# Banded attention on one core: scores and transposes in half arrays, values by pairs of key blocks, engine orders written by hand

## The chip, the cores and the metric

The kernel runs on one core of a Trainium2 chip. The metric is the device time of one execution in microseconds. The core has five engines that run at the same time: TensorE (PE, matrix products into PSUM, 8 banks of 512 fp32 columns by 128 partitions), VectorE (DVE), ScalarE (ACT), GpSimd (POOL) and SyncE (SP, which here only issues DMAs). A matmul keeps one operand in the array (the weights, which a load instruction brings in) and streams the other (the moving operand) past it.

## The reference

Two sequences (2048 and 512 rows of 1024 channels) go through an attention layer, a Fourier layer and a last RMS norm. Cut to the attention layer, which is what the change touches:

```python
def attention_layer(x, g, w_in, w_out, sink, rel_bias):
    h = rmsnorm(x, g)
    z = h @ w_in                      # q (16 heads x 64), k and v (4 heads x 64), gate (1024)
    o = banded_gqa_with_sink(q, k, v, rel_bias, sink)
    return x + (o * jax.nn.silu(gate)) @ w_out

def banded_gqa_with_sink(q, k, v, rel_bias, sink):      # blocks of 128 queries, 3 blocks of 128 keys
    scores = einsum(q, k) * scale + bias                # bias by relative position; |i - j| <= 128
    m = maximum(max(scores), sink)
    p = exp(scores - m)
    p = p / (sum(p) + exp(sink - m))
    return einsum(p, v)
```

Everything is in fp32. The kernel holds most operands as a high part, which the array's fast fp32 format keeps exactly, and a low part, the rest. A product of two such operands is three matmuls (high by high, high by low, low by high), which `matmul3` issues (lines 95 to 97).

## The kernel before

The rows are worked on in five chunks of 512 (the short sequence first). For each chunk the kernel makes the normalised and transposed input `h`, projects k and v (`kv_proj`), and then goes through 8 pairs of heads `p`. For each pair it projects q and the gate (`qg_proj`: 8 steps each, a step being one `matmul3` of 512 columns, names `qp` and `gp`) and attends (`attention`). After the last pair comes the output projection (`out_proj`, tiles `op` and `wo`). The Fourier phase follows the five chunks.

Attention of a pair goes through 4 query blocks `b` and 2 heads `j`, 64 times a chunk (`i`). For each:

- `scores` (line 436): the 128 rows of the stationary operand hold q's high part in one half and its low part in the other, so that two matmuls over 128 rows (`kwin` high, `kwin` low, the keys being held twice) make the scores of one head, 128 queries by up to 384 keys, in one of two PSUM banks `spt`. DVE adds the bias and takes the minimum of the negated scores (line 448), ACT takes the exponential and its sum (line 452), DVE the reciprocal (line 455), and DVE scales (line 458; in the first chunk ACT does so for `j` = 1, line 461).
- `transp`, `LAG` = 3 places later (line 475): up to three transposes of 128 by 128 through a PSUM tile `pt`; ACT writes the high part (line 476), DVE the low part (line 477) of the tile `pts`.
- `av`, `AVLAG` = 2 places after that (line 489): for each of up to three key blocks and for the high and the low part, a matmul of 256 columns (both heads of one query block).
- `out_evac`, once for two query blocks: ACT copies half of the result (line 497), DVE adds the halves (line 506), POOL multiplies by the gate (line 508), ACT and POOL make the high and low part of `uT` (lines 509, 510).

Between these stand the next pair's projection steps, an equal share at each place, so that TensorE has work while DVE and ACT deal with the scores. The order on an engine is the order in which the program names the instructions, as far as a scheduler leaves it; a few are tied to others with `after`. Six PSUM banks are handed out in turn (`bank`), two are `spt`. In the Fourier phase these two become a pool of their own for the accumulators W and Z.

In the first chunk the weights also come from memory in one piece and are split into high and low part on ACT (line 116) and POOL, and q and gate are scaled by the norm in PSUM (`scaled`, line 274). Later chunks read the split weights back.

## Time and profile before

| | |
|---|---|
| median of 3 runs | 1643.32 us (1642.83 to 1645.25) |
| profiled execution, its own time | 1642.68 us |
| span of its profile | 1640.9 us |
| mean granted clock of TensorE | 0.999 |
| instructions | 25865, of which 8939 matmuls |
| share of the span: PE, weight loads, DVE, ACT, POOL | 99, 85, 73, 54, 27% |
| attention stages (first to last score) | 47.1 to 185.8, 265.0 to 409.5, 482.6 to 632.6, 705.7 to 855.6, 922.6 to 1066.7 us |

The groups of the profile are named by line, engine and operation, then output tile and input tiles, the array's rows and columns, the shape, how often, the busy time, the mean length of one in ns, and the idle time before it with what ended it. A row of the order in time has the start, the length (of several equal instructions together, where it ends in x2 or more), the engine, line and tiles. Lengths of matmuls include their way through the array and overlap.

### The profile page before, as it was taken

To read this page: it belongs to the slowest core of one execution; us is meant where nothing else is said; L and a number is where in the kernel's file an instruction comes from. 1 tells how busy PE (TensorE), PEld (TensorE's weight loads), DVE (VectorE), ACT (ScalarE), POOL (GpSimd) and SP (SyncE) were. 2 spreads that over 40 slices of the span, in tenths; PEclk is the share of its full clock that TensorE was granted. 3 is DMA by queue.
4 is the path that set the end of the run, shared out by engine and by line. 5 is a ranking of instruction groups with operands and counts; after the bars stand their busy time and mean duration, and the time that the engine had idled before them with its cause. 6 is when DMAs were issued, how large, how long until landed. Compare 5 with 4: busy or idle time off the path is not lost.

```text
span 1640.9 us, 25865 instructions
## 1 busy us (share of the span) xinstructions
PE 1625.6 (99%) x8939; PEld 1400.8 (85%) x8939; DVE 1197.3 (73%) x2846; ACT 892.1 (54%) x2035; POOL 434.9 (27%) x605
## 2 busy tenths in 40 slices
PE   9999999999999999999999999999999999999998
PEld 7888888888898888988888888888888888888886
DVE  6778665888548886478783588858667667988696
ACT  6789644676236674256761467636545454343252
POOL 2457641422403313224214142121111111100010
PEclk9999999999999999999999999999999999999999
DMA  8487786574866556765648755657565469655962
GB/s 303 157 316 292 233 327 218 193 250 168 285 224 232 186 206 204 270 242 173 224 149 318 249 197 193 222 191 253 198 238 192 172 221 390 215 193 187 336 212 90
DMA packets 100637, 374.05 MB, mean 228 GB/s; under 512 B 12139, under 2 KB 22379, under 8 KB 83100
## 3 DMA queue, kind: packets, MB, share of 16 engines
q1 hardware_dynamic: 81708, 297.91, 52.7%
q0 software_dynamic: 16464, 70.30, 11.0%
q10 hardware_dynamic: 2336, 4.20, 0.7%
q8 instruction: 71, 1.16, 0.3%
q14 instruction: 58, 0.48, 0.1%
HBM read 281.10 MB, written 91.26 MB: 227 GB/s over the span
## 4 chain that ended last, share of the span: by engine, by line
PE 88%; DMA 4%; DVE 3%; ACT 2%; POOL 1%; issue 1%; SPq 0%; POOLq 0%; DVEq 0%; ACTq 0%
PE av L489 6%; PE spt L436 6%; PE pt L475 6%; PE gp L95 4%; PE gp L97 4%; PE gp L96 4%; PE qp L95 4%; PE qp L97 4%; PE qp L96 4%; PE op L95 4%; PE op L97 4%; PE op L96 4%; PE W L95 2%; PE W L96 2%; PE W L97 2%; PE fo L96 2%
## 5 line engine op out<-in xcount | busy, mean ns | idle before, releaser
L452 ACT ACTIVATE S<-S 128x385 f32<-128x385 f32 (+1 forms) x320 | 190.8, 596 | 68.9 <-DVE S L448 67.4
L477 DVE TENSOR_TENSOR pts<-pt,pts 128x384 fp32r<-128x384 f32 (+1 forms) x320 | 168.3, 526 | 41.1 <-ACT pts L476 38.8
L448 DVE CUSTOM_DVE_ANT_0 S<-spt,b 128x385 f32<-128x385 f32 (+1 forms) x320 | 168.1, 526 | 25.5 <-PE spt L436 23.3
L476 ACT CAST pts<-pt 128x384 fp32r<-128x384 f32 (+1 forms) x320 | 143.6, 451 | 76.1 <-PE pt L475 72.7
L436 PE MATMUL spt<-kwin,qab 128*128 128x384 f32 (+1 forms) x640 | 156.8, 326 | 0.0
L508 POOL TENSOR_TENSOR o<-o,s 128x256 f32<-128x256 f32 x75 | 55.4, 739 | 362.9 <-DVE o L506 361.2
L475 PE MATMUL pt<-ident,S 128*128 128x128 f32 x896 | 150.5, 273 | 0.1
L436 PEld LDWEIGHTS spt<-kwin,qab 128*128 128x128 f32 x640 | 118.3, 188 | 25.4 <-DVE S L448 0.2
L489 PEld LDWEIGHTS av<-pts,v 128*128 128x128 f32 x896 | 126.3, 189 | 13.6 <-DVE qab L382 1.3
L95 PE MATMUL gp<-h,wg 128*128 128x512 f32 x320 | 137.8, 431 | 0.0
L489 PE MATMUL av<-pts,v 128*128 128x256 f32 x896 | 136.4, 285 | 1.0 <-DVE qab L382 0.5
L95 PE MATMUL qp<-h,wq 128*128 128x512 f32 x312 | 133.7, 428 | 0.5 <-ACT wq L116 0.5
L95 PE MATMUL op<-wo,uT 128*128 128x512 f32 x320 | 126.5, 397 | 1.5 <-ACT invb L177 0.9
L475 PEld LDWEIGHTS pt<-ident,S 128*128 128x128 f32 x896 | 113.8, 140 | 14.5 <-DVE pts L477 3.4
L97 PE MATMUL gp<-h,wg 128*128 128x512 f32 x320 | 125.9, 393 | 0.0
L96 PE MATMUL gp<-h,wg 128*128 128x512 f32 x320 | 125.7, 393 | 0.0
L96 PE MATMUL op<-wo,uT 128*128 128x512 f32 x320 | 125.7, 393 | 0.0
L97 PE MATMUL op<-wo,uT 128*128 128x512 f32 x320 | 124.7, 391 | 0.0
L458 DVE TENSOR_SCALAR S<-S 128x384 f32<-128x384 f32 (+1 forms) x256 | 118.6, 463 | 7.9
L97 PE MATMUL qp<-h,wq 128*128 128x512 f32 x312 | 123.0, 394 | 0.1
L96 PE MATMUL qp<-h,wq 128*128 128x512 f32 x312 | 122.6, 393 | 0.0
L455 DVE RECIPROCAL S<-S 128x1 f32<-128x1 f32 x320 | 51.3, 160 | 65.9 <-ACT S L452 63.0
(420 smaller groups left out, 4261.0 us busy)
## 6 DMA issues: line engine op xcount, KB each, us to landing
wo<-wsd SPq DMA_DIRECT2D x32, 1024.0 KB, 5.8
wq<-wsd SPq DMA_DIRECT2D x31, 1024.0 KB, 5.1
wg<-wsd SPq DMA_DIRECT2D x31, 1024.0 KB, 6.8
x<-x1d SPq DMA_DIRECT2D x40, 512.0 KB, 3.9
b<-b21d SPq DMA_DIRECT2D x40, 512.0 KB, 5.5
b<-rowd SPq DMA_DIRECT2D x40, 384.0 KB, 4.3
xs<-in_x_dram SPq DMA_DIRECT2D x23, 512.0 KB, 6.0
s2d<-gt POOLq DMA_DIRECT2D x40, 256.0 KB, 3.7
```

Source lines behind the costliest of these rows:

```text
L95: PE.matmul(out, a[0], b[0], start=start, stop=False, skip_group_check=more)
L96: PE.matmul(out, a[0], b[1], start=False, stop=False, skip_group_check=more)
L97: PE.matmul(out, a[1], b[0], start=False, stop=stop, skip_group_check=more)
L436: PE.matmul(ps[:, 2 + k0 * P : 2 + k1 * P], q, kwin[g][:, part, b * P + k0 * P : b * P + k1 * P], start=part == 0, stop=part == 1,)
L448: DVE.tensor_tensor_reduce(out=s[:, e0:e1], in0=ps[:, 1 + e0 : 1 + e1], in1=st["bias"][:, j, 386 - e1 : 386 - e0][:, ::-1], scale=1.0, sca ...
L452: last_exp[0] = ACT.activation(s[:, e0:e1], s[:, e0:e1], AF.Exp, bias=mn, scale=-1.0, accum_out=den)
L458: DVE.tensor_scalar(s[:, ks], s[:, ks], den, None, ALU.mult)
L475: PE.transpose(ps[:, kb, :], s[:, 1 + kb * P : 1 + (kb + 1) * P], ident)
L476: ACT.copy(hi[:, k0:k1, j, :], ps[:, k0:k1, :])
L477: DVE.tensor_tensor(lo[:, k0:k1, j, :], ps[:, k0:k1, :], f32(hi[:, k0:k1, j, :]), ALU.subtract)
L489: PE.matmul(out, v, pt[:, kb].rearrange("p h q -> p (h q)"), start=kb == k0 and part == 0, stop=kb == k1 - 1 and part == 1,)
L508: eng.tensor_tensor(o, o, s, ALU.mult)
```

## The change

- A period is now two query blocks of one pair of heads, 16 to a chunk and one more to empty the pipeline. In period `n` the scores of its two blocks are made, and the transposes, values and evacuation belong to period `n` - 1.
- `scores` makes three products per head, each over 64 rows: head 0 in the first 64 rows of the array, head 1 in the other 64, in turn. q is evacuated in one piece for both heads (high part on ACT, low part on DVE). There are three `spt` banks in place of two.
- `transp` is split in halves of 64 queries: the moving operand is a 64 by 64 identity, the stationary one 64 rows of the probabilities by 128 keys. The two halves use the two halves of the array and two PSUM banks.
- On TensorE the order of a period is: scores of the first block, all half transposes of the period before, scores of the second block (these three in 64 rows), projection steps, values, projection steps.
- `av` works on both query blocks at once: the two key blocks that both of them see take matmuls of 512 columns, the outer two take 256.
- For `j` = 1 ACT does the scaling in all chunks, for `j` = 0 DVE.
- The order on PE, ACT and DVE is tied by `seq`, each instruction behind the one before it. The number of projection steps at each place is a list, `quota`.
- The pool of banks has 5 in place of 6. The first half of the output projection uses the three `spt` banks and one of the pool; k is projected into `spt`. In the Fourier phase W, Z and X share a pool of three.

The diff, cut to its core:

```diff
+    def seq(engine, ins):
+        after(ins, chain.get(engine))
+        chain[engine] = ins
+        return ins
...
-                    qa, qb = qab[:, 0], qab[:, 1]
-                    ACT.activation(qa[0:64], ps[0:64], AF.Copy, scale=-0.125)
-                    DVE.scalar_tensor_tensor(qa[64:128], ps[0:64], -0.125, f32(qa[0:64]), ALU.mult, ALU.subtract)
-                    ACT.activation(qb[64:128], ps[64:128], AF.Copy, scale=-0.125)
-                    DVE.scalar_tensor_tensor(qb[0:64], ps[64:128], -0.125, f32(qb[64:128]), ALU.mult, ALU.subtract)
+                    seq(ACT, ACT.activation(qab[:, 0], ps, AF.Copy, scale=-0.125))
+                    lo = DVE.scalar_tensor_tensor(qab[:, 1], ps, -0.125, f32(qab[:, 0]), ALU.mult, ALU.subtract)
+                    seq(DVE, lo)
...
-                    for part in range(2):
-                        PE.matmul(
-                            ps[:, 2 + k0 * P : 2 + k1 * P],
-                            q,
-                            kwin[g][:, part, b * P + k0 * P : b * P + k1 * P],
-                            start=part == 0,
-                            stop=part == 1,
-                        )
+                    for i, (qp, kp) in enumerate(((0, 0), (0, 1), (1, 0))):
+                        for j in range(2):
+                            rows = slice(64 * j, 64 * j + 64)
+                            pe(PE.matmul(
+                                banks[j][:, 2 + k0 * P : 2 + k1 * P],
+                                res["q"][rows, qp, b * P : (b + 1) * P],
+                                kwin[g][rows, kp, b * P + k0 * P : b * P + k1 * P],
+                                start=i == 0,
+                                stop=i == 2,
+                            ))
...
-                    for kb in range(k0, k1):
-                        PE.transpose(ps[:, kb, :], s[:, 1 + kb * P : 1 + (kb + 1) * P], ident)
-                    ACT.copy(hi[:, k0:k1, j, :], ps[:, k0:k1, :])
-                    DVE.tensor_tensor(lo[:, k0:k1, j, :], ps[:, k0:k1, :], f32(hi[:, k0:k1, j, :]), ALU.subtract)
+                    for j in range(2):
+                        for kb in range(k0, k1):
+                            for h in range(2):
+                                rows = slice(64 * h, 64 * h + 64)
+                                pe(PE.transpose(
+                                    ps[h][:, kb, j, :], ss[j][rows, 1 + kb * P : 1 + (kb + 1) * P], ident[rows, rows]
+                                ))
+                def parts(b):
+                    gb, k0, k1 = span(b)
+                    for h, ps in enumerate(st.pop(("pt", b))):
+                        hi, lo = (st["pts"][:, i, b % 2, k0:k1, :, 64 * h : 64 * h + 64] for i in range(2))
+                        seq(ACT, ACT.copy(hi, ps[:, k0:k1]))
+                        seq(DVE, DVE.tensor_tensor(lo, ps[:, k0:k1], f32(hi), ALU.subtract))
...
+                    todo = [(gb, slice(1, 4, 2), by_b), (gb + 1, slice(2, 5, 2), by_b)]
+                    if k0 == 0:
+                        todo.append((gb - 1, 0, out[:, :256]))
+                    if k1 == 3:
+                        todo.append((gb + 2, 5, out[:, 256:]))
+                    for n, (kb, at, to) in enumerate(todo):
+                        v = vblk[kb][:, g].rearrange("p a d -> p (a d)")
+                        for part in range(2):
+                            pt = pts[:, part].rearrange("p b k h q -> p (b k) (h q)")[:, at]
+                            pe(PE.matmul(to, v, pt, ...))
...
-                        st["ps"] = [bank(f"op{c}_{half}_{i}") for i in range(4)]
+                        st["ps"] = (spt if half == 0 else []) + [bank(f"op{c}_{half}_{i}") for i in range(3 * (1 - half), 4)]
...
+                ahead_n = 16 if c == 0 else 12
...
+                m = 15 * KD - ahead_n
+                quota = [m * (i + 1) // 27 - m * i // 27 for i in range(27)] + [3, 3, 2]
...
+                for n in range(17):
+                    new = (at[n // 2], 2 * (n % 2)) if n < 16 else None
+                    old = (at[(n - 1) // 2], 2 * ((n - 1) % 2)) if n else None
...
+                    if new:
+                        new[0].scores(new[1], spt[:2])
+                    if old:
+                        for b in range(2):
+                            old[0].transp(old[1] + b)
+                    if new:
+                        for j in range(2):
+                            new[0].biased(new[1], j)
+                        new[0].scores(new[1] + 1, (spt[2], spt[0]))
+                    if old:
+                        for b in range(2):
+                            old[0].parts(old[1] + b)
+                    if new:
+                        for j in range(2):
+                            new[0].exps(new[1], j)
+                        for j in range(2):
+                            new[0].biased(new[1] + 1, j)
+                    for i in range(quota[2 * n] if n < 15 else 0):
+                        work.pop(0)()
+                    if n >= 15:
+                        for i in range(n - 14):
+                            op.pop(0)()
+                    if new:
+                        new[0].divide(new[1], 0)
+                        for j in range(2):
+                            new[0].exps(new[1] + 1, j)
+                    if split:
+                        split()
...
+                    if old:
+                        old[0].av(old[1])
+                    if new:
+                        new[0].divide(new[1], 1)
+                        new[0].divide(new[1] + 1, 0)
+                    if old:
+                        split = old[0].out_evac(old[1])
+                    if new:
+                        new[0].divide(new[1] + 1, 1)
...
+                    if n < 15:
+                        for i in range(quota[2 * n + 1]):
+                            work.pop(0)()
+                    elif n == 15:
+                        op.pop(0)()
+                    else:
+                        split()
+                        for i in range(3):
+                            op.pop(0)()
```

More of the change, by code (lines that the diff above doesn't have):

```diff
@@ L93, in matmul3 @@
     def matmul3(out, a, b, start, stop, more=False):
-        PE.matmul(out, a[0], b[0], start=start, stop=False, skip_group_check=more)
-        PE.matmul(out, a[0], b[1], start=False, stop=False, skip_group_check=more)
-        PE.matmul(out, a[1], b[0], start=False, stop=stop, skip_group_check=more)
+        for i, j in ((0, 0), (0, 1), (1, 0)):
+            pe(PE.matmul(out, a[i], b[j], start=start and i + j == 0, stop=stop and i == 1, skip_group_check=more))
     def load_w(c, n, name, lo_engine=None, late=None):
@@ L126, in load_w @@
         return w[:, 0], w[:, 1]
[L128 removed]
+    stage, res_tile, ready, chain = [], [], {}, {}
     def after(ins, anchor):
@@ L259, in attention_phase, with zeros @@
             spt = []
-            for i in range(2):
-                s = spsum.tile([P, 512], F32, name=f"spt{i}")
-                DVE.memset(s, 0.0)
-                spt.append(s)
+            for i in range(3):
+                spt.append(spsum.tile([P, 512], F32, name=f"spt{i}"))
+            def zeros(s):
+                for cs in (slice(0, 2), slice(386, 388)):
+                    DVE.memset(s[:, cs], 0.0)
             kall = ap.tile([P, 4, 2, 768], F32R, align_bytes=LINE, name="kwin")
@@ L305, in cols @@
                     return h[0][:, c0 : c0 + n], h[1][:, c0 : c0 + n]
-                kps = [bank(f"kp{c}_{t}")[:, :n] for t in range(2)]
+                kps = [spt[1 + t][:, :n] for t in range(2)]
                 for k in range(KD):
@@ L355, in kv_proj @@
                         evac_k(t, pt[:, t * P : t * P + P], P, CH + P)
+                for t in range(3):
+                    zeros(spt[t])
                 return invb
@@ new lines, in transp @@
+                    if b % 2 == 0:
+                        st["pts"] = ap.tile([P, 2, 2, 3, 2, P], F32R, align_bytes=LINE, tag="pt", bufs=1, name=f"pts{c}_{p}_{b}")
+                    ps = st["pt", b] = [
+                        bank(f"pt{c}_{p}_{b}_{h}")[:, :384].rearrange("p (k j q) -> p k j q", k=3, j=2) for h in range(2)
+                    ]
+                    for j in range(2):
[4 more added lines that the diff above has]
+                                    ps[h][:, kb, j, :], ss[j][rows, 1 + kb * P : 1 + (kb + 1) * P], ident[rows, rows]
+                                ))
@@ L575, in out_proj @@
                 return steps
+            Heads = namedtuple("Heads", "start scores biased exps divide transp parts av out_evac")
             def pieces(out, a, b, op):
@@ L691, in attention_phase @@
             AHEAD = ahead()
-            HB = [(b, j) for b in range(4) for j in range(2)]
             tail = []
             bias = []
+            norm_steps = invb = inv = None
             def first_norms():
@@ L770, in attention_phase @@
+                chain.pop(PE)
+                if c == len(CHUNKS) - 1:
+                    for i in range(2):
+                        op[i]()
+                        op[i] = lambda: None
+                tail = op
             return tail
```

228 lines of the change are left out of this document (105 added, 123 removed).

## The prediction

> **What bounds the kernel now.** I read the page first, then the busy time by stage, then the groups of TensorE, then the order of time in one attention stage.
>
> ```profile
> span 1640.9 us, 25865 instructions
> ## 1 busy us (share of the span) xinstructions
> PE 1625.6 (99%) x8939; PEld 1400.8 (85%) x8939; DVE 1197.3 (73%) x2846; ACT 892.1 (54%) x2035; POOL 434.9 (27%) x605
> ```
> ```profile
> 47.10:185.80 138.70, 136.21 (x777) 116.94 (x776) 112.51 (x388) 119.56 (x293) 78.38 (x113) 1.00 0.67 245
> 705.70:855.60 149.90, 149.90 (x860) 130.90 (x858) 126.68 (x379) 100.39 (x252) 43.66 (x59) 1.00 0.59 198
> ```
> The two rows are the attention stages of the first and the fourth chunk (columns: length, then PE, weight loads, DVE, ACT, POOL). TensorE is busy for 149.9 of 149.9 us. DVE has 85% in the later chunk, ACT 86% in the first. So a stage is as long as the sum of TensorE's slots, and a change is worth what it takes off that sum, less the waits that it brings.
>
> Matmuls overlap: the printed length of one is not its share of the time. The share is the distance between starts.
>
> ```profile
> L475 PE MATMUL pt<-ident,S 128*128 128x128 f32 x896 | 150.5, 273 | 0.1
> ...
> L489 PE MATMUL av<-pts,v 128*128 128x256 f32 x896 | 136.4, 285 | 1.0 <-DVE qab L382 0.5 <-DVE pts L477 0.4
> ...
> L436 PE MATMUL spt<-kwin,qab 128*128 128x384 f32 x512 | 131.3, 337 | 0.0
> ...
> L436 PE MATMUL spt<-kwin,qab 128*128 128x256 f32 x128 | 25.5, 282 | 0.0
> ```
> ```profile
> 719.60 0.40 PE L97 MATMUL gp<-h,wg 128*128 128x512 f32 x1
> 719.84 0.51 PE L436 MATMUL spt<-kwin,qab 128*128 128x384 f32 x2
> 720.18 0.49 PE L475 MATMUL pt<-ident,S 128*128 128x128 f32 x3
> 720.43 0.48 PE L95 MATMUL gp<-h,wg 128*128 128x512 f32 x1
> 720.74 0.39 PE L96 MATMUL gp<-h,wg 128*128 128x512 f32 x1
> 720.97 0.40 PE L97 MATMUL gp<-h,wg 128*128 128x512 f32 x1
> ```
> The next rows, from the start of the run, are needed for 256 columns now and for more below:
>
> ```profile
> 17.21 0.39 PE L96 MATMUL kp<-h,wk 128*128 128x512 f32 x1
> 17.43 0.39 PE L97 MATMUL kp<-h,wk 128*128 128x512 f32 x1
> 17.75 1.03 PE L249 MATMUL bp<-oh,rb 33*16 33x512 f32 x2
> 18.71 0.38 PE L95 MATMUL vp<-wv,h 128*128 128x256 f32 x1
> 18.93 0.28 PE L96 MATMUL vp<-wv,h 128*128 128x256 f32 x1
> 19.05 0.28 PE L97 MATMUL vp<-wv,h 128*128 128x256 f32 x1
> ```
> Two scores last 0.51 with a mean of 0.337, so they start 0.174 apart. Three transposes last 0.49 with 0.273 each: 0.109 apart. A 512-column product follows the next after 0.23. For 256 columns (18.93 to 19.05) it is 0.12.
>
> **The change on TensorE, part by part.**
>
> Scores. Before: 512 x 0.174 + 128 x 0.12 = 104.4 us. After, a head takes three products in its own 64 rows, and the two heads of a pair stand in the two halves of the array. There are 960 matmuls, 480 pairs (384 wide, 96 narrow). If a pair costs one slot: 384 x 0.174 + 96 x 0.12 = 78.3. **-26.1 us.**
>
> Values. Before 896 x 0.12 = 107.5. After, 320 matmuls of 512 columns and 256 of 256: 320 x 0.23 + 256 x 0.12 = 104.3. **-3.2 us.**
>
> Transposes. Before 896 x 0.109 = 97.7; after 1792 halves with 64 moving columns, 896 pairs. What bounds one now is told by the one plain fp32 matmul of the trace, bp at 17.75 above, in the answer on its tile:
>
> ```profile
> L249 PE MATMUL bp<-oh,rb x2: 589/594/600, 17.8 to 18.2; 33*16 33x512 f32 x2
> ```
> Its two passes of 512 fp32 columns take 1.03 together and one 0.59, so they start 0.44 apart; a quarter of that is 0.110, the slot of a transpose. So the 128 moving fp32 columns set it, and 64 need 0.055. I take 0.06 per pair, near that end; the other end is 0.109, where the weight load of 128 columns, which the halving doesn't shorten, is the limit. 896 x 0.06 = 53.8: **-43.9 us** (-48 to 0).
>
> Switches. The new order has the 64-row work of a period in one stay: scores, 24 half transposes, scores. That is 17 stays in each of 5 chunks, so 170 switches, where before has one pair of them, at bp, which uses part of the rows. The weight loads there:
>
> ```profile
> 17.75 0.11 PEld L249 LDWEIGHTS bp<-oh,rb 33*16 33x16 f32 x2 [0.35 <-issue]
> 18.71 0.19 PEld L95 LDWEIGHTS vp<-wv,h 128*128 128x128 f32 x1 [0.85 <-ACT xs L155]
> 18.82 0.19 PEld L96 LDWEIGHTS vp<-wv,h 128*128 128x128 f32 x1
> ```
> Into it: 0.32 from the last kp to bp, against 0.23: 0.09, and its weight load started with it, not ahead (16 columns; a load of 128 prints 0.10 longer, 0.19 against some 0.09). Out of it: 18.71 - 18.19 = 0.52 against 0.44, then 0.22 against 0.12 for the first vp, whose load was not ahead: 0.18. So 0.09 to 0.19 each. I take 0.17, near the upper one, as the first loads here have 128 columns: 170 x 0.17 = **+28.9 us** (+15 to +32). The Trainium skill (TensorEngine Tiling (Array Packing), Key Properties) says that a change of tiling mode drains TensorE, and this is the rule that speaks against the change; it gives no price, and the rows here agree that there is one.
>
> Waits at the end of a chunk. In the fixed order, work is handed out as 8 projection steps to a period, but periods 13 and 14 (of 0 to 16) have 7 and 5, and in period 15 the step behind the second scores is the output projection, whose first product goes into spt0: the bank of the scores that were written last. DVE must first do two biased sums, the four low parts of the earlier transposes and two more sums:
>
> ```profile
> L448 DVE CUSTOM_DVE_ANT_0 S<-spt,b 128x385 f32<-128x385 f32 x63 | 34.9, 554 | 5.1 <-PE spt L436 4.7
> L477 DVE TENSOR_TENSOR pts<-pt,pts 128x384 fp32r<-128x384 f32 x60 | 33.2, 553 | 2.5 <-ACT pts L476 2.1
> ...
> L506 DVE TENSOR_TENSOR o<-av,t 64x256 f32<-64x256 f32 x28 | 11.7, 416 | 0.7 <-ACT t L497 0.4
> L455 DVE RECIPROCAL S<-S 128x1 f32<-128x1 f32 x62 | 10.0, 161 | 13.1 <-ACT S L452 12.5
> L393 DVE SCALAR_TENSOR_TENSOR s<-th,gp 128x512 f32<-128x512 f32 x8 | 5.5, 686 | 1.1 <-ACT th L391 1.1
> ```
> 4 x 0.554 + 4 x 0.553 = 4.4 us, in which TensorE has 12 pairs of halves (0.72), three of scores (0.52) and a switch: 1.4. It then waits 3.0. In period 14 the last gate's evacuation (0.69 on DVE) also stands in front of the next sums, with three steps fewer (3 x 3 x 0.23 = 2.1 us) to cover it: 1 more. **4 us x 5 chunks = +20** (+5 to +30: instructions of an engine overlap a little at their ends).
>
> Waits inside. ACT's queue in a period: four high parts, two exponentials, the evacuation of q or gate, two exponentials, uT, one normalising copy, the copy of av, another normalising copy.
>
> ```profile
> L452 ACT ACTIVATE S<-S 128x385 f32<-128x385 f32 x63 | 38.9, 618 | 16.9 <-DVE S L448 16.9
> L476 ACT CAST pts<-pt 128x384 fp32r<-128x384 f32 x60 | 28.1, 472 | 10.9 <-PE pt L475 10.2
> L452 ACT ACTIVATION_READ_ACCUMULATOR S<-S 128x1 f32 x63 | 11.9, 188 | 0.0
> L497 ACT COPY t<-av 64x512 f32<-64x512 f32 x14 | 8.2, 583 | 1.0 <-PE av L489 0.7
> ```
> Estimated from these, a normalising copy (384 wide, like the exponential) and an evacuation (512 wide, like the copy of av) are 0.6 each and uT (256 wide) 0.4. This makes 4 x 0.806 + 4 x 0.472 + 0.583 + 3 x 0.6 + 0.4 = 7.9 us. TensorE's period is 6 x 0.174 + 12 x 0.06 + 1.4 + 24 x 0.23 + 0.34 = 9.0. It holds, with little room where chunk 0 adds a weight's cast to each period. DVE, which gives half of its scaling to ACT, has about the same. The q evacuation halves on both (two 64-row pieces become one of 128). I put **+5 us** (0 to 10). The five banks of the pool, three banks for scores, and X of the Fourier stage in a pool of three only exchange places; the work between covers their release, 0.
>
> Sum: -26.1 - 3.2 - 43.9 + 28.9 + 20 + 5 = -19.3. The profiled execution took 1642.7 (its span of 1640.9 and 1.8 around it), 0.6 under the median of three: 1642.7 - 19.3 = 1623.4, and **1624.0** against the median.
>
> **The rivals.**
>
> *The fixed order becomes the bound* (slower). The last block's transposes need the second normalising copy, which stands behind the copy of av, two adds (0.416 each) and a reciprocal (0.161). ACT comes to the copy of av after the evacuation, two exponentials, uT and a normalising copy: 0.6 + 1.6 + 0.4 + 0.6 = 3.2 us after the first projection steps land, 1.8 after av does. From there 0.58 + 0.83 + 0.16 + 0.6 = 2.2, so it is ready 4.0 after av; TensorE gets there after 12 products (2.75), a switch and 0.52 + 0.54: also 4.0. Any ACT work in that stretch then stalls it. The first chunk has these:
>
> ```profile
> L116 ACT CAST wq<-w32q 128x1024 fp32r<-128x1024 f32 x5 | 5.2, 1046 | 0.0
> ```
> ```profile
> L274 DVE TENSOR_TENSOR gp<-gp,invb 128x512 f32<-128x512 f32 x8 | 5.5, 683 | 0.9 <-PE gp L97 0.9
> ```
> 1.05 + 0.68, of which I let 0.2 hide: 1.5 x 16 = 24 us; and half of the other 64 periods have a split of a later weight (512 wide, about 0.6, 0.4 of it bare): 13. 1624 + 37 = **1661**. It decides from 0.25 us a period on (20 / 80). Against it: instructions of ACT overlap, so 7.9 is an upper sum. Chance 0.22.
>
> *The halves' weight loads queue.* The loads above start 0.11 apart (18.71, 18.82). If two halves share that path, a pair of scores takes 0.22, 480 x 0.22 - 78.3 = +27, and a pair of transposes at least today's 0.109, +44: **1695**; at 0.22 it is +143, 1794. For it: no row shows two loads at once. Chance 0.13. The Trainium skill (TensorE: Matmul & The Clock Gate, LDWEIGHTS) says that a load's time goes by its columns and not by its rows, 107 ns for 128; by that alone, with the loads one behind the other, it would be the 1794. The Trainium skill (TensorEngine Tiling (Array Packing), Key Properties) also says that different tiles load and multiply in parallel, and then it is not. No run so far shows either.
>
> *The halves do not run side by side at all.* Scores 768 x 0.174 + 192 x 0.12 = 156.7 in place of 78.3, transposes 1792 x 0.06 = 107.5 in place of 53.8: 1624 + 132 = **1756**. Chance 0.10. That the order isn't the one described can be left out: the built program has the 170 switches and 1376 matmuls in either half.
>
> **How the numbers follow.** The forecast has 0.55; its own range is 1594 (pair 0.055, switch 0.09, ends at 2 us) to 1660 (pair 0.09). The whole range, 1594 to 1697, takes in the fixed order's case and the queue's lower price; beyond it lie the third rival and the queue's upper price. Faster by over 0.2% (3.3 us, about what a measurement can tell here): 0.50 of the forecast and 0.03 of the first rival; same 0.06; slower 0.41.
>
> **What would show it.** Right: score pairs 0.17 apart, halves of a transpose almost together and pairs about 0.06 apart, 0.1 to 0.2 around each stay, a gap of 2 to 5 us before the first output projection product into spt0. Wrong: slots of 0.17 for single scores, 0.11 for pairs of transposes, TensorE waiting in the middle chunks for ACT's normalising copies, or an attention stage that is longer than 150 us in the fourth chunk.

## The result, and the profile after

| | before | after |
|---|---|---|
| median of 4 runs each | 1644.03 us (1642.83 to 1645.25) | 1711.99 us (1707.01 to 1715.54) |
| span of the profiled execution | 1640.9 us | 1705.2 us |
| mean granted clock of TensorE | 0.999 | 0.983 |

The changed kernel is slower by 4.1% (ratio 1.0411, 95% interval 1.0383 to 1.0439). The forecast was 1624; the range ended at 1697.

The head of the page after (the last row is TensorE's granted clock in tenths of full speed, in 40 equal slices of the run):

```profile
span 1705.2 us, 27749 instructions
...
PE 1632.8 (96%) x9835; PEld 1348.5 (79%) x9835; DVE 1104.6 (65%) x2703; ACT 918.6 (54%) x2123; POOL 437.5 (26%) x605
...
PEclk9988999999999999999999999999999999999999
```

TensorE had 99% before. It now stands idle for 4% of a longer span, its clock is lower in places, and no engine beside it is busier than 65% (the weight loads are TensorE's own). So nothing ran out of throughput; something waits. The attention stages of the first and the fourth chunk (same columns as in the prediction):

```profile
42.20:205.70 163.50, 143.00 (x918) 110.61 (x917) 115.77 (x374) 113.60 (x284) 77.19 (x112) 0.93 0.58 204
751.80:898.20 146.40, 140.35 (x1017) 111.57 (x1016) 101.80 (x335) 108.15 (x272) 43.88 (x58) 1.00 0.57 200
```

In the first chunk TensorE is idle for 20 us and its clock is 0.93; in the fourth it is idle for 6 us inside the stage, where before it was idle for none. The stage itself looks 3.5 us shorter, but it holds less: the three steps of the output projection that stood inside it before (37 products, 8.5 us) now come behind the last score, against one more projection step inside (2.7 us).

A period in which nothing waits shows what the half arrays cost and bring (order of time, fourth chunk, TensorE; start, length):

```profile
807.69 0.79 PE L441 MATMUL spt<-kwin,qab 64*128 64x384 f32 x6
808.31 0.92 PE L499 MATMUL pt<-ident,S 64*128 64x64 f32 x24
809.03 0.88 PE L441 MATMUL spt<-kwin,qab 64*128 64x384 f32 x6
809.85 3.02 PE L95 MATMUL gp<-h,wg 128*128 128x512 f32 x12
812.70 1.54 PE L525 MATMUL av<-pts,v 128*128 128x512 f32 x8
814.08 2.91 PE L95 MATMUL qp<-h,wq 128*128 128x512 f32 x12
816.92 0.61 PE L441 MATMUL spt<-kwin,qab 64*128 64x384 f32 x3
```

From start to start: first scores 0.62, 24 half transposes 0.72 (0.06 a pair), second scores 0.82, projection 2.85, values 1.38, projection 2.84: 9.23 us. The halves do run side by side. A later period, 30 us on, has the waits. ACT, DVE and TensorE in it:

```profile
835.11 0.62 ACT L680 CAST e<-w32e 128x512 fp32r<-128x512 f32 x1
835.63 0.62 ACT L478 ACTIVATE S<-S 128x384 f32<-128x384 f32 x1
836.27 0.58 ACT L534 COPY t<-av 64x512 f32<-64x512 f32 x1
838.45 0.62 ACT L478 ACTIVATE S<-S 128x384 f32<-128x384 f32 x1 [1.59 <-DVE S L476]
```
```profile
837.31 0.85 DVE L543 TENSOR_TENSOR o<-av,t 64x256 f32<-64x256 f32 x2 [1.68 <-ACT t L534]
838.19 0.16 DVE L476 RECIPROCAL S<-S 128x1 f32<-128x1 f32 x1
```
```profile
836.78 0.78 PE L441 MATMUL spt<-kwin,qab 64*128 64x384 f32 x6
837.40 0.59 PE L499 MATMUL pt<-ident,S 64*128 64x64 f32 x13
838.30 0.37 PE L499 MATMUL pt<-ident,S 64*128 64x64 f32 x5 [0.31 <-DVE o L543]
839.12 0.41 PE L499 MATMUL pt<-ident,S 64*128 64x64 f32 x6 [0.45 <-ACT S L478]
```

This is one chain through three queues. ACT's cast of a later weight (835.11) holds up the copy of the values (836.27). DVE, which has nothing to do but must add before it may take the reciprocal, waits 1.68 us for that copy. ACT waits 1.59 us for the reciprocal, and TensorE's last six half transposes wait for ACT's normalising copy; five others wait for the adds, because these free the bank they write. Over the run, in the table of waits (total us, times, longest):

```profile
ACT S L478 <- DVE S L476: 101.3, 88, 3.6
DVE o L543 <- ACT t L534: 94.3, 69, 5.7
PEld pt L499 <- ACT S L478: 29.2, 61, 0.6
PE pt L499 <- DVE o L543: 12.8, 16, 1.2
PE spt L95 <- DVE S L460: 10.8, 5, 2.4
PE spt L441 <- DVE S L460: 9.9, 10, 2.0
```

For sums over the run I take the distance between the starts of successive matmuls less the slot of the first one's width, and count only waits of over 0.2 us. By that TensorE waits 46 us between transposes (77 places), 16.5 at the scores (most of it for the bank `spt0` between the two blocks, some for the low part of q), 12 before the first product of the output projection (about 2.4 in each chunk), 90 in all; before it was 11.

The clock is the second part. Before, it is 1.0 until the run's end. After, it is 0.5 in eleven stretches of 3.41 or 6.83 us, 54.6 us together, which make the slots in them longer by 17.7 us. Busy time by windows around two of them (length, PE, PEld, DVE, ACT, POOL, clock):

```profile
436.00:439.40 3.40, 0.79 (x5) 0.47 (x5) 3.40 (x13) 2.10 (x7) 0.00 (x0) 1.00 0.32 135
439.40:442.80 3.40, 3.36 (x8) 2.68 (x9) 1.13 (x7) 1.72 (x6) 0.73 (x1) 0.50 0.61 153
...
1019.66:1023.07 3.41, 1.76 (x32) 1.31 (x28) 2.13 (x8) 2.12 (x5) 3.41 (x6) 1.00 0.34 138
1023.07:1026.48 3.41, 3.41 (x12) 2.66 (x9) 2.68 (x10) 2.12 (x7) 1.59 (x3) 0.50 0.37 154
```

The first holds the wait before an output projection, the second two waits at transposes:

```profile
1021.59 0.37 PE L499 MATMUL pt<-ident,S 64*128 64x64 f32 x5 [1.19 <-DVE o L543]
1022.40 0.40 PE L499 MATMUL pt<-ident,S 64*128 64x64 f32 x6 [0.45 <-ACT S L478]
```

Behind both, TensorE works through a window at half clock.

### The profile page after: what moved, and what is told of

It reads as the page before. It is cut to its first block, busy times and chain, and to the rows that moved or that the text cites. A ratio compares the mean times of both kernels' runs of the same rounds, so it can differ in the third digit from the quotient of the medians.

```text
span 1705.2 us, 27749 instructions
## 1 busy us (share of the span) xinstructions
PE 1632.8 (96%) x9835; PEld 1348.5 (79%) x9835; DVE 1104.6 (65%) x2703; ACT 918.6 (54%) x2123; POOL 437.5 (26%) x605
## 4 chain that ended last, share of the span: by engine, by line
PE 68%; ACT 9%; DVE 8%; DMA 8%; issue 4%; POOL 2%; SPq 0%; DVEq 0%; POOLq 0%; ACTq 0%
PE spt L95 8%; PE op L95 8%; PE qp L95 8%; PE gp L95 7%; PE fo L95 6%; PE W L95 6%; PE vp L95 3%; PE z L95 3%; PE spt L441 3%; ACT S L478 3%; PE Z L95 3%; PE Wo L95 2%; PE av L525 2%; DVE o L543 2%; PE pt L499 2%
## 5 line engine op out<-in xcount | busy, mean ns | idle before, releaser
L95 PE MATMUL gp<-h,wg 128*128 128x512 f32 x960 | 244.4, 403 | 0.0
L95 PE MATMUL qp<-h,wq 128*128 128x512 f32 x960 | 241.0, 401 | 0.0
L95 PEld LDWEIGHTS gp<-h,wg 128*128 128x128 f32 x960 | 178.4, 192 | 45.1 <-issue 10.3
L95 PEld LDWEIGHTS qp<-h,wq 128*128 128x128 f32 x960 | 178.2, 191 | 42.4 <-issue 5.2
L478 ACT ACTIVATE S<-S 128x384 f32<-128x384 f32 (+1 forms) x160 | 95.0, 595 | 102.8 <-DVE S L476 101.3
L95 PE MATMUL op<-wo,uT 128*128 128x512 f32 x600 | 142.6, 389 | 0.0
L441 PE MATMUL spt<-kwin,qab 64*128 64x384 f32 (+1 forms) x960 | 129.4, 362 | 13.0 <-DVE S L460 9.9
L95 PE MATMUL fo<-wo,tTu 128*128 128x512 f32 x576 | 138.9, 392 | 0.0
L95 PEld LDWEIGHTS op<-wo,uT 128*128 128x128 f32 x600 | 112.7, 188 | 23.6
L543 DVE TENSOR_TENSOR o<-av,t 64x256 f32<-64x256 f32 x150 | 62.6, 417 | 102.2 <-ACT t L534 94.3
L95 PEld LDWEIGHTS fo<-wo,tTu 128*128 128x128 f32 x576 | 106.0, 188 | 20.2
L525 PE MATMUL av<-pts,v 128*128 128x512 f32 (+1 forms) x576 | 118.7, 345 | 2.5 <-ACT pts L507 1.9
```

The costliest lines, as they stand in the source:

```text
L95: pe(PE.matmul(out, a[i], b[j], start=start and i + j == 0, stop=stop and i == 1, skip_group_check=more))
L441: pe(PE.matmul(banks[j][:, 2 + k0 * P : 2 + k1 * P], res["q"][rows, qp, b * P : (b + 1) * P], kwin[g][rows, kp, b * P + k0 * P : b * P + k ...
L478: seq(ACT, ACT.activation(s[:, ks], s[:, ks], AF.Copy, scale=den))
L525: pe(PE.matmul(to, v, pt, start=n == part == 0, stop=part == 1 and n in (1, len(todo) - 1), skip_group_check=n > 1,))
L543: seq(DVE, DVE.tensor_tensor(o[64 * j : 64 * j + 64], ps[0:64, :, j], t2[:, :, j], ALU.add))
```

## The experiments

Three theories. **A**: the fixed orders of ACT and DVE make the normalised scores, and the banks, late for TensorE; it waits, and after waits it runs at half clock. **B**: the half arrays themselves cost more than they save. **C**: bundles of two blocks always wait for something; what is removed at one place turns up at another. The medians are each compared with runs of the kernel before on the same chip (1643.4 to 1644.7).

**Each cause by itself, first four.** The last normalising copy goes ahead of the values' evacuation in ACT's and DVE's order:

```diff
+                    if new:
+                        new[0].divide(new[1] + 1, 1)
                     if old:
                         split = old[0].out_evac(old[1])
-                    if new:
-                        new[0].divide(new[1] + 1, 1)
```


> The changed kernel with one move: the last normalising copy of a period stands ahead of the evacuation of the values, so that it waits no longer for the copy of av and the two adds. Theory A (the fixed order of ACT and DVE is late for the transposes, and TensorE's waits then halve its clock): most of the 46 us that the transposes of the changed kernel wait inside their runs go, and with them some of the half-clock stretches: 1640 to 1670 us. Theory B (work in half arrays is itself slow, the waits are a by-product): within 10 us of 1712. Theory C (order in general: any fixed order gives as much waiting elsewhere): 1690 to 1710, with the waits moved to av or the scores.

1697.01 us (1.0333, 1.0305 to 1.0361): 15 us better. Waits between transposes fell from 46 to 40 us and those between scores from 16.5 to 9.4, but now the transposes wait for a bank:

```profile
PEld pt L499 <- ACT pts L507: 29.6, 28, 1.8
```

The chain is real, but turning the order round makes the copy of the values late, and DVE's adds with it (in this run they wait 131 us for it). Both neighbours are needed at the same time.

The output projection later in the last period (the moved calls are not shown), and its banks in another order:

```diff
-                quota = [... // 27 ... for i in range(27)] + [3, 3, 2]
+                quota = [... // 28 ... for i in range(28)] + [2, 3, 3]
...
-   st["ps"] = (spt if half == 0 else []) + [bank(...)]
+   st["ps"] = [bank(...)] + (spt[1:] + spt[:1] if half == 0 else [])
```


> The changed kernel with another end of a chunk: projection steps last into period 15, the output projection starts behind the values of period 15, and its first product goes into a bank of the pool, spt0 last. Theory A: the waits for spt in period 15 (some 2.4 us before the output projection and 2 before the second scores, five times) fall to under 1.5 us a chunk, and the half-clock stretch after each chunk (3.4 to 6.8 us at half speed) goes: 20 to 35 us less, 1677 to 1692. Theory B: no change, as the waits are short of what work in half arrays costs.

1710.89 us (1.0412): no gain. The waits before the output projection went, but with the projections handed out more thinly each q is ready just before it is needed, and the scores wait for its evacuation:

```profile
PEld spt L441 <- ACT qab L388: 51.2, 32, 5.0
```

This one is theory C's.

TensorE's order kept, ACT's and DVE's left to the scheduler:

```diff
     def seq(engine, ins):
+        if engine is not PE:
+            return ins
```


> The changed kernel with the ties on ACT and DVE left out; those on TensorE stay. Theory A, if the ties are at fault: the scheduler puts instructions that are ready ahead, 1640 to 1680 us. If it is the order in which the program names them, ties or not: 1695 to 1715, the same waits. Theory B: 1700 to 1715.

1681.25 us (1.0231, 1.0207 to 1.0255): 31 us of the 68 came from these two orders. Waits between transposes fell to 11 us; those of the values for DVE's low parts rose to 12. Half-clock stretches went from 54.6 to 27.3 us, and the five that were left stood at the five chunks' ends.

Order, banks and values kept, but scores and transposes over all 128 rows, with q in its old layout and evacuated in two pieces on each engine:

```diff
-  for i, (qp, kp) in enumerate(((0, 0), (0, 1), (1, 0))):    # 64 rows, both heads in turn
+  for j in range(2):
+      for part in range(2):                                  # 128 rows, as before the change
...
-  pe(PE.transpose(ps[h][:, kb, j, :], ss[j][rows, ...], ident[rows, rows]))
+  pe(PE.transpose(ps[j][:, kb, :], ss[j][:, ...], ident))
```


> The changed kernel's periods, ties, banks and values by pairs of key blocks, but with scores and transposes over all 128 rows as before the change (two matmuls a head, full transposes, q in its old layout). TensorE's slots per period are then some 0.45 us longer, 34 us over the run. Theory A (the order is at fault, the half arrays pay): the waits stay but shrink by what the longer slots cover: 1700 to 1735 us. Theory B (half arrays are at fault): 1640 to 1665 us.

1746.66 us (1.0625, 1.0604 to 1.0646). The half arrays are worth 35 us in this order, so theory B falls: they pay, and the order loses more than they bring. Not all of the 35 us are TensorE's slots: by the reckoning above this run also waits some 9 us longer.

**Chunk ends, values and clock.** In the next, ACT and DVE are free and the first half of the output projection begins with the row block that stands in a bank of the pool; its weights are asked for a period earlier, and `spt0` is used last (both not shown):

```diff
+ pairs = [(3, k) for k in range(4)] + [(i, k) for k in range(4) for i in range(3)]
+ pairs += [(i, k) for k in range(4, KD) for i in range(4)]
...
- for i in range(4):
+ for i, k in pairs[4 * n : 4 * n + 4]:
```


> The kernel with the order of ACT and DVE left free (1681), and in the first half of the output projection the twelve products of the row block in the pool's bank over the first four heads stand ahead of the first product into the scores' banks; their weights are asked for one period earlier. Theory A (TensorE's waits, and the half clock that follows them, are what is lost): the five waits between the last scores and the output projection (14.0 us) and the five stretches at half clock behind them (27.3 us of stretches, 8.4 us of longer slots) go, so 1681 - 18 to - 22 = 1659 to 1663. Theory C (a wait of that size turns up at another place whatever is moved): within 5 us of 1681, with the 14 us shown elsewhere.

1669.24 us (1.0151): 12 us, not the 18 to 22 expected. The 14.0 us of waits fell to 0.9 and the half-clock stretches from 27.3 to 13.7 us, 3.4 of these in the Fourier phase. One new wait of some 2.6 us came later in the output projection of the first chunk, with a stretch at half clock.

On top of that, five projection steps and not four ahead of the values, and in the values all high parts first:

```diff
+ for i in range(0, 26, 2):
+     quota[i], quota[i + 1] = quota[i] + 1, quota[i + 1] - 1
...
- for n, (kb, at, to) in enumerate(todo):
-     for part in range(2):
+ for part in range(2):
+     for n, (kb, at, to) in enumerate(todo):
```


> As the run before, and five projection steps of a period instead of four stand ahead of the value products, which take all upper parts before all lower parts. Theory A: the 20 waits inside the value products (12.2 us) mostly go and 10 us come off, 1650; with the 11.3 us of waits at the transposes unchanged. Theory C: the transposes wait longer since less work stands between the second scores and them, or projections wait for banks, and the time is within 3 us of the run before.

1672.6 us (1.0167): no gain. The waits inside the values went (12.6 us to under 1), and those between transposes rose from 11 to 32: theory C again. Values that come later are evacuated later.

Work without effect in the wait, in the changed kernel:

```diff
+ if half == k == 0:
+     for _ in range(12):
+         pe(PE.matmul(st["ps"][3], uTs[0][0][:, :P], hi[:, :512], start=True, stop=True))
```


> The changed kernel, with twelve further matmuls of 128x512 (2.7 us at full clock) ahead of the first product of each output projection, into the pool's bank, whose content the first product then overwrites: work that fills the wait and adds nothing to the output. If the half clock follows from TensorE standing idle (theory A), the wait of 2.3 to 2.6 us is filled, the five stretches at half clock behind it go with some 8 us of longer slots, and the time falls to about 1704 although work was added. If the clock falls for another reason (a rhythm of its own, or the amount of work), the stretches stay and the time is 1712 to 1715.

1703.68 us (1.0355, 1.0338 to 1.0373), against 1711.99: 8 us less in the median with 60 matmuls more, as the clock's part of theory A said. All four runs lie below all four of the changed kernel, but the two profiled executions are only 1.7 us apart (1705.3, the slowest of its four, and 1707.0, the fastest). The stretch shown above is gone; the same place in this run, from the start of the wait on:

```profile
435.80:439.20 3.40, 2.14 (x29) 1.43 (x27) 1.84 (x5) 2.14 (x7) 0.73 (x1) 1.00 0.61 171
439.20:442.60 3.40, 3.02 (x15) 2.40 (x16) 3.40 (x14) 2.10 (x7) 0.00 (x0) 1.00 0.33 140
```

The expectation was too simple in one point: at three of the five chunk ends a stretch stayed, behind the waits between the scores that stand ahead of the filled one. All stretches together fell from 54.6 to 41 us, though some came at new places.

No ties at all:

```diff
     def seq(engine, ins):
-        after(ins, chain.get(engine))
-        chain[engine] = ins
         return ins
```


> The changed kernel with all ties between instructions left out, TensorE's too, so that the planner places periods, values and projections by its own due times (it puts three projection steps ahead of the values and four behind). Theory A (fixed places are the loss): at least the 31 us that the free ACT and DVE gave, 1670 to 1681. Theory C: the bundles of two blocks wait wherever they stand, 1681 to 1700.

1665.99 us (1.0141, 1.0124 to 1.0158), 46 us better than with all ties and a little better than the forecast band. The scheduler's own places beat the written ones, but not the kernel before.

The same with the row block first and the high parts first:

> No ties, the row block of the output projection that needs no scores' bank first, and the value products take all upper parts before all lower ones. Theory A: against the kernel without ties (1666) the 16 us of waits inside and before the value products shrink by 8 to 12 us, as the lower part, which comes last, is needed 0.7 us later, and the last waits of the output projection (2 us) go: 1653 to 1657. Theory C: the time is within 3 us of 1666 and the waits stand before the transposes instead.

1667.24 us (1.0143): no gain. Waits inside the values 13.3 to 2.4 us, between transposes 11 to 19. Theory C's outcome, in a free order.

**The chain cut.** DVE's adds, which stand between ACT's copy and the reciprocal, go to POOL; ACT copies both halves to SBUF for it, and the tile `o` has one buffer in place of two. The last values of a chunk stay as they were:

```diff
+ t1 = ap.tile([64, 2, 2, P], F32, tag="t1", bufs=1, ...)
+ seq(ACT, ACT.copy(t1, ps[0:64]))
...
- seq(DVE, DVE.tensor_tensor(dst, ps[0:64, :, j], t2[:, :, j], ALU.add))
+ POOL.tensor_tensor(dst, t1[:, :, j], t2[:, :, j], ALU.add)
```

Without ties, on top of the last run:

> As the run before, and the two additions of each pair of blocks' values leave DVE: ACT copies both halves of the bank to SBUF (0.6 us more on ACT a period) and GpSimd adds them (two additions of some 0.7 us). It takes 0.84 us a period off DVE and, with it, the place at which the reciprocals stand behind an addition that waits for ACT. If DVE's queue is what makes the normalised scores late (theory A's chain), the waits before transposes (11 us) and values fall to less than a half and the time is 1640 to 1650. If ACT is as close to its limit as DVE (rival), it is 1655 to 1670.

1729.34 us (1.0515): far outside both expectations. In the scheduler's order the values now wait for ACT, in 52 places, and ACT in its turn stands still for POOL:

```profile
PEld av L523 <- ACT pts L505: 55.1, 52, 1.9
ACT uT L553 <- POOL o L550: 139.9, 68, 2.7
```

ACT's cast of `uT` needs POOL's product, and what follows on ACT is late with it: at 352.94 us, for one, ACT has stood idle for 2.69 us ahead of that cast, and an exponential and the copies of the transposes come behind. In the run without this edit ACT waited 100 us there; with the two additions ahead of the product it waits 140. That this makes up the whole loss is not shown.

With all ties, in the changed kernel and nothing else:

> The changed kernel with all its ties, and only the additions moved off DVE as in the run before: ACT's order then has a second copy between the copies of the transposes and the last normalising copy. If the chain seen in the middle chunks (ACT's copy of the values, DVE's additions, the reciprocal, the normalising copy, the transposes) costs what the waits before the transposes show (46.3 us and a part of the 17.7 us of slots at half clock), some 25 to 45 us come off: 1667 to 1687. If the second copy on ACT takes the place of the additions in the chain, 1700 to 1712.

1667.05 us (1.0133, 1.0116 to 1.0149): **45 us** from this one edit, the upper end of what theory A gave. Of the two rows that led the excerpt above, the normalising copy's 101.3 us fall to 4.7 and the adds' 94.3 are gone; TensorE's waits at the transposes fall from 46 to 16 us. The weight loads' waits at the output projection and at the transposes are now

```profile
PEld spt L95 <- DVE S L460: 13.2, 5, 2.8
...
PEld pt L499 <- ACT t L537: 8.1, 12, 0.9
PEld pt L499 <- ACT S L478: 7.4, 27, 1.0
```

The same edit is worth -45 us in the fixed order, where ACT's cast of `uT` stands late enough to wait 5 us in all, and +62 in the free one. It also takes 0.84 us of work a period off DVE; that the order and not this work is what counts is supported by the run with ACT and DVE free (31 us with the same work) and by a later one that gives DVE a copy back.

With it, the row block first (two repairs), and in the other run also the last normalising copy ahead of the values' copies and the high parts first:

> All ties kept, and of these repairs only two: the additions off DVE and the row block that needs no scores' bank first. Theory A: 1667 less the 12.6 us of waits before the output projection and 8 to 11 us of slots at half clock: 1643 to 1647. If the normalising copy's place matters beside it, it stands 5 to 10 us above the run with all three; if not, the two are level within 3 us. Theory C: 1655 to 1667.

> All ties kept; the additions off DVE, the last normalising copy ahead of the values' copies on ACT, the value products with all upper parts first, and the row block of the output projection that needs no scores' bank first. Theory A: the three repairs act on different waits, so from 1667 the waits before the output projection (12.6 us) go with the slots at half clock behind them (8 to 11 us), and half of the 16.4 us before the transposes: 1636 to 1646, level with the kernel before (1644) or ahead of it by up to 0.5%. Theory C: what is taken away at one place turns up at another, 1650 to 1667.

1654.48 us (1.0067, 1.0048 to 1.0087) and 1654.05 us (1.0069, 1.0054 to 1.0083). The row block is worth 13 us, less than the 20 to 24 expected. The place of the normalising copy, tried together with the high parts first, is worth nothing once the adds are gone: in the run with it ahead, the transposes wait for the bank of the values in its stead (24.0 us against 8.1 in the run with the adds gone):

```profile
PEld pt L499 <- ACT t L537: 24.0, 32, 1.4
```

The six runs with two repairs (adds and row block) spread from 1645 to 1659; the profiled one, the lowest, has one stretch at half clock (6.8 us) before the run's end. In it the last period of a chunk still shows a wait between the two scores, 1.0 us in the fourth (ACT, DVE, TensorE):

```profile
847.90 0.62 ACT L478 ACTIVATE S<-S 128x384 f32<-128x384 f32 x1
848.42 0.58 ACT L396 ACTIVATE th<-gp 128x512 f32<-128x512 f32 x1
```
```profile
849.10 0.69 DVE L398 SCALAR_TENSOR_TENSOR s<-th,gp 128x512 f32<-128x512 f32 x1 [3.13 <-ACT th L396]
849.70 0.55 DVE L460 CUSTOM_DVE_ANT_0 S<-spt,b 128x385 f32<-128x385 f32 x1
```
```profile
850.32 0.79 PE L441 MATMUL spt<-kwin,qab 64*128 64x384 f32 x5 [1.00 <-DVE S L460]
```

DVE has been idle for 3.13 us, but the last gate's evacuation stands ahead of the biases that free `spt0`. So the third repair puts it behind them:

```diff
+ if n == 15:
+     res[7]["late"]()        # evac_g of the last pair, behind the second scores' biases
```


> The run with two repairs, and in the last period of each chunk the evacuation of the last gate (tanh on ACT, one step on DVE, which wait for ACT's last normalising copy) stands behind the biases of the second scores instead of ahead of those of the first. Theory A: the waits between the two blocks' scores in that period (1.0 to 2.2 us in each of five chunks, 8 us of the 12.2) go: 1645 to 1648 against 1654. Theory C: the output projection or the values of that period wait for the bank that the gate now holds longer, within 3 us of 1654.

**1644.46 us** (ratio 1.0002, 0.9992 to 1.0012): level with the kernel before. Its profile has one stretch at half clock, 3.4 us. Two attempts to go on from there. In the first, DVE and not ACT makes the second copy of the values' bank:

> As the run before, and the second copy of the values' bank is DVE's (one copy of 64x512, no wait for ACT) instead of ACT's, so that one copy and not two stands ahead of ACT's last normalising copy. Theory A (the normalising copy late behind the values' copies is what is left): the waits before the transposes (16.4 us) fall to less than a half, 1636 to 1643, ahead of the kernel before (1644). Rival: DVE is again late with the reciprocal behind the copy, and the time is that of the run before or up to 5 us above it.

1664.67 us (1.0123): the rival's side, and worse than it. DVE's copy waits for ACT's in 69 places (71 us), though it needs nothing of it; both read the same bank, and what ties them was not settled. The reciprocal is behind that wait again, and the waits at transposes are 33 us.

In the second, the last normalising copy of a period is DVE's:

> The kernel with three repairs (additions off DVE, the row block first, the last gate's evacuation behind the biases), and the last normalising copy of each period is DVE's multiplication (0.42 us) instead of ACT's copy (0.62 us), so that it no longer stands behind ACT's two copies of the values. Theory A: the waits of transposes for that copy (8.7 us) go and those for the values' bank stay: 1633 to 1640, ahead of both kernels. Rival: what stands behind it on DVE (the biases, which free the scores' bank) is late by as much, and the time stays within 3 us of 1644.

1643.47 us (0.9999, 0.999 to 1.0009): no gain over the run with three repairs. The weight loads' wait for the normalising copy fell from 7.8 to 2.4 us, and one of 3.4 us for DVE's multiplication came in its place; 8.8 us for the values' bank stay. No version was faster than the kernel before.

## Why the prediction was wrong, point by point

- **Scores, values, transposes** (-26.1, -3.2, -43.9): right. A pair of scores takes a slot (0.17 us), a pair of half transposes 0.06 us. The two rivals of the array (queued weight loads, halves one after the other) did not come: 24 half transposes start in 0.72 us, each with a weight load of 138 ns. The Trainium skill (TensorEngine Tiling (Array Packing), Key Properties) says that different tiles load and multiply in parallel; the trace agrees, and the 1794 that one queue of loads would have made is refuted.
- **Switches** (+28.9): too small. A free period took 9.23 us and not 9.0, with 0.10 more in the first scores, 0.30 in the second and 0.08 to 0.09 in each stretch of projections, some 0.55 a stay in place of 0.34. 85 stays x 0.21 = +18 us more.
- **Chunk ends** (+20, 4 us each): right in kind and near in size by itself. 2.0 to 2.4 us of idle time at the output projection and 1.2 between the scores of the last period, by the rows of the five chunks. Its two repairs brought 13 and 10 us.
- **Waits inside** (+5): the step that failed. At the transposes alone TensorE waited 46 us. The prediction summed ACT's work (7.9 us of a period of 9.0) and found that it fits, but a queue that fits can still be late, since each engine stood still for the other: DVE's adds for ACT's copy, ACT's copy for DVE's reciprocal. Cutting that chain alone brought 45 us.
- **First rival** (the fixed order becomes the bound; 1661, chance 0.22): its mechanism is what happened, chain and all, weight casts included. Its price was 37 us; the edit that cuts the chain measured 45, and that these are near each other is in part luck: it put 24 us into the first chunk and 13 into the others, and only about a third of the waits at the transposes stand in the first. It had worked out the copy's readiness and TensorE's arrival both at 4.0 us, so no slack at all, and still gave this case 0.22. It missed that the adds also hold the bank that the transposes write (12.8 us in 16 places): the prediction had put the pool of five banks at nothing. What this pool, and the one buffer of `pts` in place of two, cost by themselves was not tried.
- **Two bounds** do not follow from the terms beside them: a pair at 0.055, a switch at 0.09 and ends of 2 us give 1596 and not 1594, a pair at 0.09 gives 1651 and not 1660.
- **Not foreseen: the clock.** The prediction took each wait at its length and had no term for the clock. Eleven stretches at half clock added 17.7 us. The Trainium skill (TensorE: Matmul & The Clock Gate, Part 1) describes a gate that halves TensorE's clock after a window of some 3.4 us with too little activity; the trace agrees on the window.

The sum with the measured terms closes: 1624 without the 25 us that it had put in for waits is 1599; + 18 for the switches; + 79 of waits (90 less the 11 of before) + 17.7 of slots at half clock = 1714, against 1711.99 measured. That it meets the median so closely is luck: waits and clock are read from the profiled execution, which took 1707.0, so the sum is 7 us too long for it. For the version with three repairs the same sum has 30 us of waits more than before (41 in all) and 1.4 at half clock: 1648 against 1644.46. Without them it would stand near 1617 by this estimate; how many of these a better order could still remove stays open.

## What to carry to other kernels

Adding up an engine's work in a period says whether it keeps up, not whether it is on time: write down, for each result that another engine waits for, what stands ahead of it in the queue and what that waits for in turn. In a hand-written order, work that waits for another engine (here the adds behind a copy) must not stand ahead of something urgent, even on an engine that is a third idle. When a wait is removed at one place, look for it at the next before going on; of the edits tried here, moving the normalising copy or the values within the order only moved the wait, while taking the adds out of the chain removed it in the written order. The same edit made a longer wait in the scheduler's order, so it has to be read against the queue that takes the work over.

## What the runs showed of the hardware

- The granted clock changes on a grid of 3.41 us: all starts of stretches in a run lie on multiples of it from one another. In the changed kernel all eleven windows that had full clock and were followed by half clock had TensorE busy for at most 0.57 of their length; of its other windows at full clock only one was below 0.60 (0.54). In the other runs the two kinds overlap between 0.44 and 0.65.
- No single long gap is needed. The window at 1019.66 has none longer than 1.2 us and was followed by half clock. The Trainium skill (TensorE: Matmul & The Clock Gate, Why this matters for your kernels) warns of idle gaps of over some 3 us; here two waits of 1.19 and 0.45 us in one window were enough.
- The spread between runs can go with the clock: the six runs with two repairs lie 14 us apart, and the mean granted clock is 0.996 in the two shortest and 0.991 to 0.993 in the three longest. That the price of a wait depends on where in a window of the grid it falls would explain this, but is not shown; the kernel before, with a clock of 0.997 to 0.999, spread by 2.4 us in four runs and by 7 in seventeen.
- Changing between 128 and 64 rows shows in the table of waits as weight loads that come late though they wait for nothing that the profile shows ("issue"):

```profile
PEld spt L441 <- issue: 19.4, 55, 0.4
PEld gp L95 <- issue: 10.3, 39, 0.4
```

  In the run over 128 rows the first row has no counterpart, and the second is 0.3 us in one place. On TensorE it shows as longer distances: 0.09 us ahead of the first scores, 0.10 more within them, 0.30 more within the last scores and 0.10 in the first product behind them.
